# Top-sixteen selection by quarter of the sequence, the first quarter's beside the mixer's last quarter

## The chip, the cores and the metric

The kernel runs on one core of a Trainium2 chip. The metric is device time in microseconds (us), as the median of several runs. Five engines work side by side, each through its own instruction queue in order: TensorE (PE, matmuls), VectorE (DVE), ScalarE (ACT), GpSimd (POOL) and SyncE (SP), whose queue issues the DMA transfers.

## The reference

Two layers over a sequence of 1040 real columns (16 learned ones and 1024 inputs, width 1024). Each layer adds a mixer and then PEER, an expert network with product keys.

```python
for i in range(DEPTH):                       # DEPTH = 2
    h = h + hybrid_mixer(rms_norm(h, attn_norm[i]), ...)
    h = h + peer_ffn(rms_norm(h, ffn_norm[i]), ...)
return rms_norm(h[:, BLOCK:], final_norm)

def peer_ffn(xn, wq, sub_keys, u, v):
    q = (xt @ wq).reshape(t, PEER_HEADS, 2, PEER_HALF)          # 8 heads, two halves
    s = einsum('thpd,hpnd->thpn', q, sub_keys)                  # 64 scores for each head and half
    s_top, i_top = top_k(s, 16)
    cand_s = s_top[:, :, 0, :, None] + s_top[:, :, 1, None, :]  # sums of pairs
    best_s, best_j = top_k(cand_s, 16)
    g = softmax(best_s)
    h_all = einsum('td,nd->tn', xt, u)                          # all 4096 experts
    a = gelu(h_sel) * g                                         # h_sel: the 128 chosen ones of h_all
    w = zeros(t, 4096).at[arange(t), idx].add(a)
    return w @ v
```

The mixer is a sliding-window attention, a stick-breaking attention and a gated linear attention beside each other, each with a norm of its own, and an output projection.

## The kernel before

Matmuls run in a split of float32: each operand is a rounded part and a remainder, and a product takes three matmuls. A piece of weights that is used for the first time is copied by ACT (L272) and its remainder formed on POOL or DVE (L279, by the list that `split_on` set last); a piece that was kept comes back by DMA, with one ACT copy (L306).

The columns are cut in quarters of 272, 256, 256 and 256 (in layer 1 the first has 256 too). The mixer goes quarter by quarter (`attn_span`, in it `sbreak` with the scans L715 and the products L718, then `out_span`). PEER then works on two pairs of quarters, P (the first two) and Q (the last two). For a pair:
- `scores` (L977) gives the scores in four blocks c of two heads each; ACT moves them out of PSUM (L982).
- `route_steps` selects on DVE for the whole pair, one c after the other. `top16` is five instructions: maximum, index, replace, maximum, index (L994 to L998). It runs once for each tile of up to 128 columns, head and half of the keys (80 groups in P of layer 0, which has five tiles; 64 where there are four), and once for each tile and head on the sums of pairs (40 or 32 groups). Some thirty further instructions for each c turn positions into expert numbers and gates (an Exp on ACT, L1029; the products L1064 and L1067; the last steps L1079 to L1082). In the text the second top-sixteen and these are "the combination".
- `slots` transposes the result on PE (L1120, L1121, L1125); it needs all four c of the pair.
- `hidden` makes h_all row by row, 32 rows (L1101, with Gelu on ACT, L1110). `gates` (DVE L1140 to L1145, PE L1152) builds gates for 16 columns at a time; it needs the slots and is spread over the rows from `PR` = 17 on.
- `values` multiplies with v in two passes of 32 rows (L1191; operands by ACT L1185 and DVE L1186), then `hupdate` (L259) adds to h. During P's values, Q's scores and selection are mixed in, by a budget for each row (`BUD`, `EVERY`).

P's first-quarter scores for three of the four c in layer 0 (two in layer 1: `P.ns` is 4 there, and 3 of them) are issued in the mixer's last quarter, but selection on DVE starts only behind the mixer's last post-processing, `A.done`: the DVE instruction L598 of the last quarter.

A scheduler sets the order of the instructions of each engine when the program is built; the engines then keep to it. So an instruction that waits holds up what stands behind it on its engine. Tiles lie at fixed places in two large buffers, `arena` and `arena_r`, and the scheduler keeps those that overlap apart. While the mixer's last quarter runs, `widen` gives some of its tiles second or third buffers, in a place that the projections of earlier quarters no longer need.

## Time and profile before

| | us |
|---|---|
| median of 3 runs | 3345.01 |
| lowest and highest | 3344.48, 3348.84 |
| profiled execution | 3347.21 |
| its span in the trace | 3345.5 |
| PE busy | 3140.4 |
| DVE busy | 2107.7 |
| ACT busy | 1311.3 |
| POOL busy | 938.1 |

The profile is of one execution. Its own time is 1.7 us more than the span, which lies around the first and the last instruction. Busy times of the engines overlap. Times in the rows further down count from the span's start.

### The profile page before, as it was taken

How to read it: one execution, taken by the hardware profiler on the slowest of the kernel's cores; microseconds unless marked ns; L12 is line 12 of the kernel's file. 1: busy time of each engine (PE TensorE's matmuls, PEld its weight loads, DVE VectorE, ACT ScalarE, POOL GpSimd, SP SyncE). 2: the span in 40 equal slices, each digit the busy share in tenths (PEclk: the TensorE clock that was granted, in tenths of full speed). 3: DMA queues.
4: the chain of work that ended last, by engine and by line, in shares of the span. 5: the costliest groups of instructions: out<-in, count | busy, mean ns of one | idle time of the engine just before them, and what ended most of it. 6: DMA issues, size and time to landing. Idle time of an engine off the chain costs nothing.

```text
span 3345.5 us, 65752 instructions
## 1 busy us (share of the span) xinstructions
PE 3140.4 (94%) x23483; PEld 2642.3 (79%) x23483; DVE 2107.7 (63%) x6764; ACT 1311.3 (39%) x3021; POOL 938.1 (28%) x963
## 2 busy tenths in 40 slices
PE   7999999989799989999998999999898899999998
PEld 7686887679799988888875868876776778688788
DVE  4645436569997589653325464465697867975447
ACT  4544324433223434324344343245342244333345
POOL 4314021214344233010311131223143433311125
PEclk9899999989899999999997999999898999999999
DMA  8767774655335655446874677756754366554655
GB/s 290 228 208 245 238 261 135 199 188 187 124 117 158 183 178 190 155 152 200 311 251 151 216 263 238 253 160 201 233 177 139 115 181 219 182 187 145 194 177 160
DMA packets 397225, 651.36 MB, mean 195 GB/s; under 512 B 43536, under 2 KB 109152, under 8 KB 396896
## 3 DMA queue, kind: packets, MB, share of 16 engines
q1 hardware_dynamic: 396896, 647.16, 60.1%
q8 instruction: 184, 3.01, 0.4%
q14 instruction: 145, 1.19, 0.1%
HBM read 489.56 MB, written 157.42 MB: 193 GB/s over the span
## 4 chain that ended last, share of the span: by engine, by line
PE 61%; DVE 21%; DMA 6%; ACT 2%; issue 2%; POOL 1%; SPq 0%; DVEq 0%; POOLq 0%; ACTq 0%
PE b L1191 15%; PE b L1101 14%; PE b L333 11%; PE b L977 4%; PE b L1152 3%; PE b L703 2%; DVE arena_r L1186 2%; DMA arena<-h 2%; DVE arena L995 2%; DVE arena L996 2%; PE b L757 1%; DVE arena L998 1%; PE b L618 1%; DVE arena L1140 1%; DVE arena L1145 1%
## 5 line engine op out<-in xcount | busy, mean ns | idle before, releaser
L279 POOL TENSOR_TENSOR arena_r<-arena,arena_r 128x512 fp32r<-128x512 f32 (+1 forms) x453 | 557.6, 1238 | 915.0 <-ACT arena_r L272 843.8
L1101 PE MATMUL b<-arena_r 128*128 128x512 f32 (+2 forms) x3840 | 766.4, 359 | 22.9 <-ACT arena L1110 13.4
L1191 PE MATMUL b<-arena_r 128*128 128x512 f32 (+2 forms) x4224 | 752.5, 337 | 31.9 <-DVE arena_r L1186 22.1
L1191 PEld LDWEIGHTS b<-arena_r 128*128 128x128 f32 x4224 | 642.6, 190 | 128.9 <-DVE arena_r L1186 37.2
L1101 PEld LDWEIGHTS b<-arena_r 128*128 128x128 f32 x3840 | 630.7, 193 | 123.0 <-ACT arena L1110 14.0
L333 PE MATMUL b<-arena_r 128*128 128x256 f32 (+1 forms) x4992 | 700.9, 294 | 27.5 <-ACT arena_r L272 6.3
L333 PEld LDWEIGHTS b<-arena_r 128*128 128x128 f32 x4992 | 641.0, 195 | 67.1 <-issue 20.4
L272 ACT ACTIVATE arena_r<-arena 128x512 fp32r<-128x512 f32 x456 | 285.0, 629 | 447.3 <-PE b L1101 93.7
L1186 DVE TENSOR_TENSOR arena_r<-arena,arena_r 128x512 fp32r<-128x512 f32 (+2 forms) x352 | 258.1, 743 | 215.6 <-ACT arena_r L1185 214.8
L306 ACT ACTIVATE arena_r<-arena 128x512 fp32r<-128x512 f32 x284 | 178.5, 631 | 359.8 <-PE b L1191 118.0
L977 PE MATMUL b<-arena_r 128*128 128x256 f32 (+1 forms) x1632 | 219.1, 290 | 17.9 <-DMA arena_r<-m_0l 6.4
L977 PEld LDWEIGHTS b<-arena_r 128*128 128x128 f32 (+1 forms) x1632 | 204.2, 190 | 30.9 <-DMA arena_r<-m_0l 8.5
L1140 DVE TENSOR_TENSOR arena<-arena 128x2048 f16<-128x2048 f16 x129 | 172.4, 1338 | 59.7 <-PE b L1152 59.7
L1108 POOL TENSOR_TENSOR arena<-arena 128x272 f32<-128x272 f32 (+26 forms) x86 | 90.0, 1051 | 372.5 <-ACT arena L1159 177.5
L1185 ACT ACTIVATE arena_r<-arena 128x512 fp32r<-128x512 f32 (+2 forms) x352 | 171.8, 502 | 24.1 <-PE b L1191 24.1
L1152 PEld LDWEIGHTS <-arena 128*128 128x128 f16 x4128 | 144.9, 118 | 36.9 <-DVE arena L1145 20.8
L1152 PE MATMUL b<-arena 128*128 128x32 f16 x4128 | 154.0, 190 | 18.9 <-DVE arena L1145 18.8
L255 POOL TENSOR_TENSOR arena<-arena 128x256 f32<-128x256 f32 (+2 forms) x105 | 90.7, 864 | 260.5 <-ACT arena L254 256.0
L715 DVE TENSOR_TENSOR_SCAN arena<-arena,zf 128x384 f32<-128x384 f32 (+6 forms) x116 | 104.5, 904 | 82.0 <-ACT arena L710 81.0
L279 DVE TENSOR_TENSOR arena_r<-arena,arena_r 128x256 fp32r<-128x256 f32 (+1 forms) x187 | 98.0, 528 | 89.7 <-ACT arena_r L272 72.0
L421 ACT ACTIVATE arena<-b 128x256 f32<-128x256 f32 (+1 forms) x144 | 55.4, 385 | 212.3 <-PE b L333 211.8
L1157 DVE SCALAR_TENSOR_TENSOR arena<-b,arena 128x288 f32<-128x288 f32 (+21 forms) x129 | 63.7, 499 | 111.6 <-PE b L1152 111.6
(268 smaller groups left out, 3877.9 us busy)
## 6 DMA issues: line engine op xcount, KB each, us to landing
arena<-in_v_w_dram SPq DMA_DIRECT2D x288, 256.0 KB, 2.9
arena<-in_u_pk_dram SPq DMA_DIRECT2D x256, 256.0 KB, 3.0
arena_r<-a_0h SPq DMA_DIRECT2D x108, 256.0 KB, 3.6
arena_r<-a_0l SPq DMA_DIRECT2D x108, 256.0 KB, 3.9
arena_r<-a_1h SPq DMA_DIRECT2D x108, 256.0 KB, 3.0
arena_r<-a_1l SPq DMA_DIRECT2D x108, 256.0 KB, 3.5
arena<-m SPq DMA_DIRECT2D x92, 256.0 KB, 4.4
arena<-in_w_pk_dram SPq DMA_DIRECT2D x72, 256.0 KB, 4.3
```

What stands on the lines that cost most here:

```text
L272: ACT.activation(hi, src, AF.Copy)
L279: e.tensor_tensor(lo[:, a:b], src[:, a:b], hi[:, a:b].bitcast(F32), op=ALU.subtract)
L306: ACT.activation(hi, wload(src), AF.Copy)
L333: PE.matmul(ps, wt[:, ks], x.at(low, k, xo, sp.w), start=(k == 0 and i == 0), stop=(k == KT - 1 and i == 2))
L715: DVE.tensor_tensor_scan(keep[0:m, 0:wd][:, ::-1], keep[0:m, 0:wd][:, ::-1], zf[0:m, 0:1].to_broadcast([m, wd]), keep[0:m, wd:wd + 1], op0 ...
L977: PE.matmul(ps, yv(half, low, k, oo, m), wt[:, kk * 256:kk * 256 + 256], start=(k == 0 and i == 0 and e == 0), stop=(k == KT - 1 and i == ...
L1101: PE.matmul(ps, wt[:, ks], yv(h, low, k, 0, w // 2 if h is None else w), start=(k == 0 and i == 0), stop=(k == KT - 1 and i == 2))
L1140: DVE.tensor_tensor(Lh, iotaM.unsqueeze(1).to_broadcast([128, 4, 128, 4]), v4(P.mT, 128), op=ALU.is_equal)
L1152: PE.matmul(ps[:, i * 32:(i + 1) * 32], Lh[:, b, :, t], R[:, b, part, :, t], start=(part == 0), stop=(part == 1))
L1185: ACT.activation(ah, G[:, r, o:o + w], AF.Copy)
L1186: last = DVE.tensor_tensor(al, G[:, r, o:o + w], ah.bitcast(F32), op=ALU.subtract)
L1191: PE.matmul(ps, wt[:, d * 128:d * 128 + 128], pr[low], start=(opens and r == 0 and i == 0), stop=(closes and r == 31 and i == 2))
```

## The change

It does these things:
- `route_steps` becomes `tops` (the first top-sixteen) and `combine` (the second and all that follows). Both work on one half of a pair (one quarter) and on two of the four c at once (`cc`), so that a call has 12 or 8 groups in place of 10 or 8, and `NG` is 12.
- All of the first quarter's scores, and `tops` on them, are issued in the mixer's last quarter, ahead of `out_span`. They have a place of their own (`s0`, `V`, `I`), where `widen` had the mixer's extra buffers; `widen` now adds one tile `sel` and nothing else.
- `combine` of the first quarter follows `A.done`; the second quarter's `tops` and `combine` come behind its scores. `slots` is called for each half, and `gates` reads the half's own tiles.
- ACT moves two tiles of scores out of PSUM in one instruction. The rings of PSUM banks for hidden, gates and scores are changed.
- In P's values, Q's scores stand at rows 6, 12, 18 and 24 of the first pass, both norms at row 0; the selection's budget is 2.4 for each row of the first pass and 1.8 for the second, with the steps priced anew. Of Q's second half only `tops` are in it; its `combine` follows the first `HQ` = 8 (was 6) rows of Q's hidden, and gates are spread up to row 31 (`PEND`, was 29).
- `hload`, `hsq` and `hupdate` work by quarter. Layer 0's last values no longer put every fourth remainder on DVE. At the end of the kernel the final norm of the first three quarters is placed inside the value passes, and only the last quarter stays in SBUF.

```diff
-    wide = [("sel", 2), ("pc", 1), ("pp", 1), ("pmt", 1), ("osq", 1)]
     def widen():
-        o = place["qaT0"][1][0]
-        for t, n in wide:
...
+        place["sel"][1].append(o_in)
...
+    o1 = lay(1, [("s0", 1536, 1), ("V", 384, 2), ("I", 384, 2)], place["qaT0"][1][0])
...
+    def tops(P, half, cc):
+        nt = len(P.parts[half][1].tiles)
...
+        for a in range(8):
+            for j in range(nt):
+                top16(sv(P, half, 2 * cc + a // 4)[:, j, a % 4, :], V[:, j, a], I[:, j, a])
+                yield 1.3
+
+    def combine(P, half, cc, startT, pidxT):
+        nt = len(P.parts[half][1].tiles)
+        ng = 4 * nt
+        V, I = P.V.pop((half, cc))
...
             if q == 3:
-                for c in range(P.ns - 1):
-                    scores(l, P, c, (0,), "d")
+                for cc in range(2):
+                    for c in (2 * cc, 2 * cc + 1):
+                        scores(l, P, c, (0,), "d")
+                    run(tops(P, 0, cc))
                 rb = rstd(2 * l + 1, qs[1])
             out_span(l, L, A)
...
-        scores(l, P, P.ns - 1, (0,), "s")
         apply(2 * l + 1, qs[1], gf, Y[1], rb)
...
-        for c in range(P.ns):
+        with tc.issue_after(A.done):
+            run(combine(P, 0, 0, *tabs), combine(P, 0, 1, *tabs))
+        for c in range(4):
             scores(l, P, c, (1,), "s")
-            with tc.issue_after(A.done):
-                route(P, c, startT, pidxT)
+        slots(P, 0)
+        run(tops(P, 1, 0), combine(P, 1, 0, *tabs))
         hidden(l, P, G, 0, 4, "h")
...
+        run(tops(P, 1, 1), combine(P, 1, 1, *tabs))
+        slots(P, 1)
         hidden(l, P, G, 4, PR, "h")
-        slots(P)
         hidden(l, P, G, PR, 32, "h", cst, PEND)
...
+        work = {6 * c + 6: lambda c=c: scored.append(scores(l, Q, c, (0, 1), "g")) for c in range(4)}
+        work[0] = norms
+        todo = values(l, P, G, (0, 1), 0, select(), work, 2.4)
+        todo = values(l, P, G, (0, 1), 4, todo, (), 1.8)
+        run(todo)
         hidden(l, Q, G, 0, HQ, "h")
-        slots(Q)
+        run(combine(Q, 1, 0, *tabs), combine(Q, 1, 1, *tabs))
+        slots(Q, 1)
```

In the changed kernel `top16` is L996 to L1000 (was L994 to L998), the hidden matmuls L1113 (was L1101), the slots' transposes L1131, L1132 and L1136 (were L1120, L1121 and L1125), and the values' DVE operand L1197 (was L1186). Three places show the move.

DVE, layer 0, inside the last quarter of the mixer, before: scans and products of the stick-breaking attention with copies out of PSUM between them.

```order
L715 SCALAR_TENSOR_TENSOR arena<-arena,zf 128x512
L747 COPY arena<-b_69 128x512
L718 SCALAR_TENSOR_TENSOR arena<-arena 128x512
L715 SCALAR_TENSOR_TENSOR arena<-arena,zf 128x272
L718 SCALAR_TENSOR_TENSOR arena<-arena 128x272
L715 SCALAR_TENSOR_TENSOR arena<-arena,zf 128x400
```

The same stretch with the change, on the same engine:

```order
L1000 MAX_INDEX arena<-arena 128x8 x4
L715 SCALAR_TENSOR_TENSOR arena<-arena,zf 128x384
L1000 MAX_INDEX arena<-arena 128x8
L587 TENSOR_TENSOR arena<-arena,b_71 128x256
L1000 MAX_INDEX arena<-arena 128x8
L279 TENSOR_TENSOR arena_r<-arena,arena_r 128x256
L996 MAX arena<-arena 128x8
L718 SCALAR_TENSOR_TENSOR arena<-arena 128x384
L996 MAX arena<-arena 128x8 x3
L588 TENSOR_TENSOR arena<-arena 128x256
L997 MAX_INDEX arena<-arena 128x8 x4
L715 SCALAR_TENSOR_TENSOR arena<-arena,zf 128x272
```

All 240 instructions of the first quarter's first top-sixteen (48 groups) now stand ahead of `A.done`, and 160 (32 groups) in layer 1.

PE, layer 1, hidden rows of P around the transposes of the second quarter's slots, before; a row of hidden is 24 matmuls, and the rows above this place bring the hidden matmuls ahead of the first L1120 to 409 of 768.

```order
L1101 MATMUL b_72<-arena_r 128x512 x24
L1101 MATMUL b_65<-arena_r 128x512 x24
L1125 MATMUL b_67<-ident,arena 128x128
L1101 MATMUL b_66<-arena_r 128x512
L1120 LDWEIGHTS arena
L1120 MATMUL b_68<-ident_78,arena 128x128
L1101 MATMUL b_66<-arena_r 128x512
```

The same place with the change, where the count ahead of the first L1131 of the second half is 243:

```order
L1113 MATMUL b_68<-arena_r 128x512 x24
L1136 MATMUL b_65<-ident,arena 128x128
L1113 MATMUL b_71<-arena_r 128x512 x24
L1113 MATMUL b_72<-arena_r 128x512 x4
L1136 MATMUL b_65<-ident,arena 128x128
L1113 MATMUL b_72<-arena_r 128x512 x20
L1113 MATMUL b_67<-arena_r 128x512 x3
L1131 LDWEIGHTS arena
L1131 MATMUL b_66<-ident_78,arena 128x128
```

The transposes have moved 166 hidden matmuls forward on PE; in layer 0 they have moved from 816 of 1536 narrower ones to 510.

DVE, layer 1, from the last operand of P's values on, before:

```order
L1186 TENSOR_TENSOR arena_r<-arena,arena_r 128x512
L994 MAX arena<-arena 128x8 x4
L995 MAX_INDEX arena<-arena 128x8
L994 MAX arena<-arena 128x8 x3
L1058 COPY arena<-arena 128x8
L1059 TENSOR_TENSOR arena<-arena 128x15x8
L995 MAX_INDEX arena<-arena 128x8 x4
```

And with the change:

```order
L1197 TENSOR_TENSOR arena_r<-arena,arena_r 128x512
L996 MAX arena<-arena 128x8 x13
L997 MAX_INDEX arena<-arena 128x8
L996 MAX arena<-arena 128x8
L997 MAX_INDEX arena<-arena 128x8 x7
L1039 COPY arena<-arena 128x8
L997 MAX_INDEX arena<-arena 128x8 x4
```

Between this operand and Q's last slots DVE had 15 groups of top-sixteen and now has 40, in both layers; on PE the hidden matmuls of Q ahead of the first L1120 or of the second half's first L1131 were 174 and are 279 (278 in layer 0).

## Rows read from the trace of the kernel before

**Rows 1.** The page: engine busy times, and the group of remainders on POOL.
```profile
PE 3140.4 (94%) x23483; PEld 2642.3 (79%) x23483; DVE 2107.7 (63%) x6764; ACT 1311.3 (39%) x3021; POOL 938.1 (28%) x963
...
L279 POOL TENSOR_TENSOR arena_r<-arena,arena_r 128x512 fp32r<-128x512 f32 (+1 forms) x453 | 557.6, 1238 | 915.0 <-ACT arena_r L272 843.8
```

**Rows 2.** Windows: length; busy of PE, PEld, DVE, ACT, POOL; clock; DMA.
```profile
642.00:699.00 57.00, 50.87 (x372) 35.39 (x371) 31.92 (x65) 22.99 (x51) 11.99 (x26) 0.95 0.31 97
699.00:910.00 211.00, 179.57 (x1358) 174.35 (x1359) 194.05 (x1153) 69.68 (x139) 75.11 (x57) 0.92 0.56 183
910.00:1045.00 135.00, 129.40 (x1766) 127.40 (x1766) 114.86 (x149) 37.16 (x108) 65.47 (x49) 0.96 0.35 111
...
2290.00:2355.50 65.50, 60.68 (x484) 45.48 (x480) 37.17 (x75) 28.76 (x63) 23.25 (x35) 0.97 0.47 158
2355.50:2546.00 190.50, 160.63 (x838) 136.29 (x837) 167.54 (x960) 66.97 (x118) 66.07 (x52) 0.90 0.62 203
2546.00:2684.00 138.00, 123.13 (x1392) 102.81 (x1392) 105.64 (x141) 37.60 (x93) 61.73 (x42) 0.91 0.36 116
```

**Rows 3.** PE's waits, 680 to 1310: us in total, times, longest.
```profile
PE b L1191 <- DVE arena_r L1186: 11.1, 19, 1.6
PE b L1120 <- DVE arena L1080: 7.8, 1, 7.8
```

**Rows 4.** PE's waits, 2330 to 2960.
```profile
PE b L1152 <- DVE arena L1145: 13.3, 8, 3.0
PE b L1120 <- DVE arena L1080: 9.1, 1, 9.1
...
PE b L1191 <- DVE arena_r L1186: 7.6, 7, 2.2
```

**Rows 5.** DVE's timeline: `A.done` of each layer, and parts of top16.
```profile
698.18 0.69 DVE L598 TENSOR_TENSOR arena_r<-arena,arena_r 128x512 fp32r<-128x512 f32 x1 [0.76 <-ACT arena_r L597]
...
701.15 0.07 DVE L995 MATCH_VALUE_LOAD arena<-arena 128x8 f32 x1
...
702.70 0.07 DVE L995 MATCH_VALUE_LOAD arena<-arena 128x8 f32 x1
...
2354.90 0.69 DVE L598 TENSOR_TENSOR arena_r<-arena,arena_r 128x512 fp32r<-128x512 f32 x1 [0.76 <-ACT arena_r L597]
...
2355.90 1.22 DVE L994 MAX8 arena<-arena 128x8 f32<-128x64 f32 x9
```

**Rows 6.** DVE's waits, 699 to 910.
```profile
DVE arena L373 <- DMA arena<-h: 8.0, 3, 3.9
```

**Rows 7.** PE's timeline in P's hidden: start, us, idle before in brackets.
```profile
765.16 23.57 PE L1101 MATMUL b<-arena_r 128*128 128x272 f32 x192
...
908.29 0.19 PE L1120 MATMUL b<-ident,arena 16*128 16x16 f16 x1 [7.83 <-DVE arena L1080]
...
2426.38 72.47 PE L1101 MATMUL b<-arena_r 128*128 128x512 f32 x312
...
2544.91 0.29 PE L1120 MATMUL b<-ident,arena 128*128 128x128 f16 x1 [9.08 <-DVE arena L1080]
...
2567.52 2.31 PE L1152 MATMUL b<-arena 128*128 128x32 f16 x64
2569.68 5.58 PE L1101 MATMUL b<-arena_r 128*128 128x512 f32 x23
...
2683.73 6.48 PE L1191 MATMUL b<-arena_r 128*128 128x512 f32 x15 [1.56 <-ACT arena_r L1185]
```

**Rows 8.** One copy of the combination by form, 2355 to 2546 and 2690 to 2960.
```profile
L1080 DVE COPY arena<-arena 128x128 f16<-128x128 f16 x4 | 4.6, 1154 | 0.0
...
L1080 DVE COPY arena<-arena 128x128 f16<-128x128 f16 x3 | 1.4, 457 | 0.0
```

**Rows 9.** Timelines of DVE and PE, from P's last values to Q's slots, layer 1.
```profile
2923.21 0.87 DVE L1186 TENSOR_TENSOR arena_r<-arena,arena_r 128x512 fp32r<-128x512 f32 x1
...
2967.33 0.23 PE L1120 MATMUL b<-ident,arena 128*128 128x128 f16 x1
```

**Rows 10.** Windows: the first projection of layer 1.
```profile
1604.00:1690.00 86.00, 76.52 (x513) 69.64 (x513) 26.66 (x49) 32.43 (x64) 37.69 (x37) 0.96 0.97 344
```

More of the change, by code (lines that the diff above doesn't have):

```diff
@@ L1111, in hidden, with slots @@
             P.rows = r + 1
-            while cst and P.gated < P.sp.w and P.gated * (end - lo) < P.sp.w * (r + 1 - lo):
-                gates(P, G, *cst)
-    def slots(P):
-        sp = P.sp
-        for j, (o, m) in enumerate(sp.tiles):
+            while cst and sum(P.gated) < P.sp.w and sum(P.gated) * (end - lo) < P.sp.w * (r + 1 - lo):
+                gates(P, int(P.gated[0] == P.parts[0][1].w), G, *cst)
+    def slots(P, half):
+        for j, (o, m) in enumerate(P.parts[half][1].tiles):
             tp = ps1("g").bitcast(F16)[:, 0:256].rearrange("p (a b) -> p a b", a=2)
@@ L1305, in tile_trunk @@
-        work += [lambda c=c: scores(l, Q, c, (0, 1), "d") for c in range(4)]
-        step = 0
-        done = []
-        for d in (0, 4):
-            for last in values_steps(l, P, G, (0, 1), d):
-                done.append(last)
-                step += 4
-                if work and step >= EVERY:
-                    work.pop(0)()
-                    step = 0
-                    if len(work) < 4:
-                        todo = itertools.chain(todo, route_steps(Q, 3 - len(work), startT, pidxT))
-                if len(work) < 4:
-                    left = BUD * 4
-                    with tc.issue_after(done[-1 - LAG]):
-                        while left > 0:
-                            left -= next(todo, 9)
@@ L1322, in tile_trunk, with norms, select @@
-        for _ in todo:
-            pass
-        split_on(POOL)
+        Q = peer_setup(qs[2], qs[3], False)
+        scored = []
+        def norms():
+            apply(2 * l + 1, qs[2], gf, Y[0], rb)
+            apply(2 * l + 1, qs[3], gf, Y[1], rb2)
+        def select():
+            for half in range(2):
+                for cc in range(2):
+                    for gen in (tops(Q, half, cc), combine(Q, half, cc, *tabs) if half == 0 else iter(())):
+                        while len(scored) < 2 * cc + 2:
+                            yield 99
+                        yield from gen
+                if half == 0:
+                    slots(Q, 0)
@@ L1344, in tile_trunk, with final @@
             continue
-        hs = sb([128, KT, 512], F32, "s")
-        for k in range(KT):
-            SP.dma_start(hs[:, k], hv[2 * l + 1][k][:, Q.sp.c0:Q.sp.c1])
-        values(l, Q, G, (0, 1), 0, hs)
-        split_on((POOL, DVE))
-        for sp in qs[0:2]:
+        def final(sp):
             rb = rstd(2 * DEPTH, sp)
```

264 lines of the change are left out of this document (137 added, 127 removed).

## The prediction

> **What bounds the kernel now.** I read the page first, then busy times by stretch, PE's waits, and the timelines around those waits. PE is busy for 3140.4 us of the 3345.5 [rows 1], so only its idle time and its clock can give much. In PEER the idle time lies around P's selection: PE is idle for 31 us of the 211 between the mixer's end and the slots of layer 0, and for 30 of the 190 in layer 1 [rows 2]. In those two stretches DVE is busy for 194 and 168 us: selection bounds them. PE could run hidden rows ahead, but its order puts the transposes at a fixed place, and there it stands and waits, 7.8 us in layer 0 and 9.1 in layer 1, for the last steps of the combination [rows 3, 4]. Behind the slots PE bounds (129.4 us busy of 135, and 123.1 of 138) [rows 2], except that in layer 1 the last gates come one by one behind the last hidden row, for which PE waits 13.3 us [rows 4].
>
> So P's end is a chain of three: `A.done`; from there DVE's work up to the slots; then what PE still has to do behind the slots. The change touches all three.
>
> **A.done.** It stands at 698.9 and 2355.6 (start and length of L598) [rows 5]. 48 groups of top-sixteen come ahead of it in layer 0 and 32 in layer 1. A group's price: a load of match values with its index or replace takes (702.70 - 701.15) / 8 = 0.194 us, a maximum 1.22 / 9 = 0.136 [rows 5], so three of the first and two of the second make 0.85 us. That is 41 and 27 us. The stretch before `A.done` had 31.9 us of DVE work in 57, and 37.2 in 65.5 [rows 2]. In layer 0, 31.9 + 41 = 73 is 16 more than fits; I take **18 later**. In layer 1, 37 + 27 = 64 would just fit, but only if the order left no hole, and the scans wait for ACT and PE in between; I take **9 later**. Bounds: 16 and 0 if every hole is filled, 41 and 27 if none is. Score matmuls that move into the mixer lay behind `A.done` before; they are not new work for PE. The loss of the extra mixer buffers is within these bounds: it makes holes.
>
> **From A.done to the slots.** The stretch loses these groups: 194 - 41 = 153 us of DVE work in layer 0 and 168 - 27 = 140 in layer 1. Before, DVE also idled there, 17 and 23 us [rows 2]; 8.0 of it in layer 0 was the load of h for the norm [rows 6], while top-sixteen of the first quarter waited its turn behind. The combination of a quarter that is already scored can lie under these loads, so I take 2 and 3 us of idle: **155 and 143**. Bounds: 153 and 140 with none; 170 and 163 with all the old idle. PE can keep up: 510 hidden matmuls at 23.57 / 192 = 0.123 us are 63 us in layer 0, 243 at 72.47 / 312 = 0.232 are 56 in layer 1 [rows 7].
>
> **Behind the slots.** The price of earlier slots is that more of hidden is left. Layer 0: 1536 - 510 = 1026 matmuls at 0.1228 = 126 us, and 33 blocks of gates with 32 matmuls at (2569.68 - 2567.52) / 64 = 0.0338 [rows 7] = 36; with 2 us of small waits, **164**. Layer 1: 525 at 0.2323 = 122, and 32 blocks = 35; with 2, **159**. The gates now run to row 31 among hidden matmuls, so the 13.3 us of waiting has no place; that is in these numbers. Before, the same pieces were 1045 - 908 = 137 and 2684 - 2545 = 139 [rows 2, 7].
>
> Together: layer 0 ends P's hidden at 698.9 + 18 + 155 + 164 = 1036 against 1045, **-9**; layer 1 at 2355.6 + 9 + 143 + 159 = 2666.6 against 2683.7, **-17**.
>
> **Values of P.** PE waits there for its low operand (L1186), 11.1 and 7.6 us [rows 3, 4], which queues on DVE behind pieces of selection. With the change less selection lies in these passes (below), so I take **-14** of the 18.7; bounds 0 and -18.7.
>
> **Q's second half.** What leaves the values comes behind them. From the last L1186 of P's values to Q's slots DVE took 44 us (2923.21 to 2967.33), and PE 174 x 0.2323 = 40 us of hidden and about 4 of values; nobody waited [rows 7, 9]. With the change DVE has 25 more groups (21 us), about half as much again of the other steps (12 by the ratio of their number) and two gate blocks (4): 44 + 37 = 81. PE now has 279 matmuls ahead, 65 + 4 = 69. So a new wait of 12 at most appears; DVE's 44 may hold some idle time, so I take 8 in each layer, **+16** (bounds 0 and +24). This is where the stall goes.
>
> **The rest.** The first projection of layer 1 loses DVE's share of its remainders. POOL was busy for 37.7 of these 86 us [rows 10], at 1.24 us for each [rows 1]; every fourth one in the layer's last values falls to it too. POOL stays below half full on average, but pieces come in bursts: **+3**, between 0 and +8. More and smaller loads and updates of h, ACT's merged score copies, the banks and the final norms inside the values lie under PE-bound values and POOL's 72% of idle time [rows 1]: **0**; without that cover the last norm alone could cost about 3.
>
> **Sum** against the profiled execution: 3347.2 - 9 - 17 - 14 + 16 + 3 = 3326 (3325.3 unrounded). The profiled run is 2.2 us over the median of those shown, so **3323**.
>
> **Two rules against the trace.** The same 128x128 copy of the combination took 1154 ns between 2355 and 2546 and 457 later in the values [rows 8]. The Trainium skill, "GPSIMD Engine Reference", section 8, Key points, says that GpSimd shares its interfaces to SBUF with VectorE and contends with some of its instructions; by that rule the moved selection is as slow beside POOL's work in the mixer as before. The trace agrees that the price depends on the stretch, and in layer 1 POOL works in 35% of the old selection and of the mixer's last quarter alike [rows 2], so the sum stays as it is. The clock in P's stretches was 0.90 to 0.92 where PE idled most and 0.95 to 0.97 where it idled less [rows 2]. The Trainium skill, "TensorE: Matmul & The Clock Gate", HAM oscillation, warns that pauses between bursts bring the lower clock back. The trace's clocks agree; since one pause before the slots stays and the late gates' pauses go, I put it at 0, between -8 and +8.
>
> **The rivals.**
> *More is gained.* Q's slots don't wait, the values lose all 18.7, and the combination leaves no hole: 3323 - 16 - 5 - 5 = 3297. If three steps of each of the four combinations also cost 0.7 us less, as in the values [rows 8], 17 more over both layers: 3280. For it: DVE idles a third of the time [rows 1]. Against it: Q's count of matmuls.
> *Nothing is gained.* DVE's order has holes again: the second quarter's scores come only after the norm, and what stands behind a waiting instruction waits as well. All the old idle time costs 15 + 20 = 35 us: 3358; half of it, about 3339. For it: 17 and 23 us of idle were there before although work was at hand [rows 2]. Against it: the combination needs nothing from the second quarter.
> *Slower.* The mixer's last quarter is serialised: with single buffers and top-sixteen in DVE's queue ahead of the scans, none of the moved 68 us fits into holes. Then `A.done` is 41 and 27 later, 41 more than I take: 3364. It decides from a total delay of about 27 + 22 = 49 us. For it: DVE's order stands fixed and the scans' chain runs over DVE, ACT and PE; against it: 25 and 28 us of DVE idle time lie in these stretches [rows 2].
>
> **How the numbers follow.** Forecast (3305 to 3338) 0.52; more gained (3280 to 3305) 0.18; nothing gained (3338 to 3358) 0.17; slower (3355 to 3385) 0.13. A measurement of this kernel tells 0.2%, or 6.7 us, from no change. Faster than 3338.3: the first two, 0.70. Within: most of the third and a little of the fourth, 0.14. Slower: the rest, 0.16. The range 3284 to 3348 leaves out 0.2, most of it above.
>
> **What would show it.** After: `A.done` near 717 and 2365; the last transposes of the second half 155 and 143 us later; no gates behind the last hidden row; values from about 1036 and, from `A.done`, 302 us later in layer 1; a wait of some 8 us for DVE at Q's second slots. The forecast is wrong if the mixer's last quarter grows by more than 25 us in a layer, if DVE idles over 10 us before the slots, or if the values' operand waits stay.

## The result: slower by 0.65%

The changed kernel took 3369.05 us (median of 4 runs, 3366.37 to 3373.87) against 3346.93 for the kernel before on the same chip (4 runs). The ratio is 1.0065 with a 95% interval of 1.0046 to 1.0084. The profiled span grew from 3345.5 to 3372.2 us, by 26.7. On other chips the kernel before had medians of 3350.9 to 3353.1 us, so experiments are compared below by their ratio to it on the same chip, and by stages of their profiles. A profile is one execution; a stage of one kernel repeats within some 5 us.

The page of the changed kernel says at first sight that nothing happened: PE has the work of before, DVE 40 us less, in a longer span.

```profile
PE 3139.0 (93%) x23453; PEld 2643.3 (78%) x23453; DVE 2067.2 (61%) x6737; ACT 1309.9 (39%) x3005; POOL 946.3 (28%) x966
```

The loss has to be read by stages. I took them from the timelines, each from the start of the first instruction to the start of the next stage's first; "third A.done" is that of the mixer's third quarter.

| stage | before | after | change | forecast |
|---|---|---|---|---|
| layer 0: third `A.done` to the last | 142.8 | 169.2 | +26.4 | +18 |
| to P's values | 347.2 | 319.6 | -27.5 | -27 |
| P's values, to their last matmul | 261.0 | 255.9 | -5.1 | -7 |
| to Q's values | 216.5 | 228.3 | +11.8 | +8 |
| to layer 1's third `A.done` | 700.0 | 708.2 | +8.1 | +3 |
| layer 1: to the last `A.done` | 132.1 | 153.7 | +21.6 | +9 |
| to P's values | 328.8 | 308.5 | -20.4 | -26 |
| P's values | 246.1 | 240.2 | -5.8 | -7 |
| to Q's values | 213.6 | 225.2 | +11.6 | +8 |
| to the end | 202.1 | 207.7 | +5.7 | 0 |

The rows of the changed kernel that answer to `A.done` in [rows 5], on DVE's timeline:

```profile
724.90 0.69 DVE L598 TENSOR_TENSOR arena_r<-arena,arena_r 128x512 fp32r<-128x512 f32 x1 [0.76 <-ACT arena_r L597]
...
2390.53 0.69 DVE L598 TENSOR_TENSOR arena_r<-arena,arena_r 128x512 fp32r<-128x512 f32 x1 [0.76 <-ACT arena_r L597]
```

And those that answer to [rows 2], windows with the columns given there, cut at the new `A.done`, the second half's first transposes and the start of P's values:

```profile
642.00:725.60 83.60, 70.64 (x508) 53.28 (x505) 73.25 (x455) 29.80 (x61) 15.46 (x33) 0.91 0.38 114
725.60:876.00 150.40, 121.95 (x896) 117.69 (x895) 145.87 (x778) 49.12 (x98) 49.84 (x35) 0.89 0.60 194
876.00:1044.50 168.50, 166.57 (x2086) 165.03 (x2087) 114.33 (x138) 48.30 (x134) 80.46 (x61) 0.98 0.42 134
2284.00:2391.00 107.00, 94.83 (x693) 66.06 (x689) 81.45 (x362) 47.02 (x101) 31.16 (x43) 0.93 0.52 164
2391.00:2529.00 138.00, 114.03 (x627) 98.78 (x626) 134.00 (x712) 47.44 (x86) 42.64 (x34) 0.88 0.63 205
2529.00:2699.00 170.00, 158.86 (x1555) 132.26 (x1554) 111.82 (x134) 49.15 (x116) 81.78 (x59) 0.96 0.46 144
```

In layer 0, DVE's 73.25 us of work in the mixer's last stretch are the 31.9 of [rows 2] and the 41 of the moved groups, and the stretch that held 57 us is now 83.6 long. Behind it selection is as short as forecast (150.4 us, DVE busy for 145.9). But add PE's idle time over the three stretches: before 6.1 + 31.4 + 5.6 = 43 us, now 13.0 + 28.5 + 1.9 = 43. It has only moved. What layer 0 gained behind `A.done` it had paid ahead of it. The windows of layer 1 do not begin at the same place (67 us behind the third `A.done` in [rows 2], 47 here), but the whole way from the third `A.done` to P's values says the same of both layers: PE is idle for 50.8 us before and 52.3 after in layer 0, and for 55.2 and 54.1 in layer 1.

The rows that answer to [rows 7] and [rows 9], PE's timeline: the transposes of the second half, the last gates of layer 1, the start of P's values, and Q's first hidden rows.

```profile
876.21 0.23 PE L1131 MATMUL b<-ident,arena 128*128 128x128 f16 x1 [2.14 <-DVE arena L1092]
...
1044.52 1.67 PE L1203 MATMUL b<-arena_r 128*128 128x272 f32 x12
...
1299.73 0.96 PE L1203 MATMUL b<-arena_r 128*128 128x256 f32 x7
1310.08 2.50 PE L1113 MATMUL b<-arena_r 128*128 128x512 f32 x5 [9.40 <-DVE arena L259]
...
2529.34 0.23 PE L1131 MATMUL b<-ident,arena 128*128 128x128 f16 x1 [0.31 <-DVE arena L1092]
...
2692.35 1.25 PE L1164 MATMUL b<-arena 128*128 128x32 f16 x32 [1.73 <-DVE arena L1157]
2695.98 1.24 PE L1164 MATMUL b<-arena 128*128 128x32 f16 x32 [2.38 <-DVE arena L1157]
2699.00 1.22 PE L1203 MATMUL b<-arena_r 128*128 128x512 f32 x2 [1.77 <-ACT arena_r L1196]
...
2949.41 2.08 PE L1113 MATMUL b<-arena_r 128*128 128x512 f32 x4 [2.94 <-DVE arena L259]
```

Q is late by the forecast's amount and more, but not at the slots: PE stands for 9.40 us at Q's first hidden row and waits for an update of h. The forecast has no such wait.

### The profile page after: what moved, and what is told of

Read it like the earlier page. It is cut to its first block, busy times and chain, and to the rows that moved or that the text cites. A ratio compares the mean times of both kernels' runs of the same rounds, so it can differ in the third digit from the quotient of the medians.

```text
span 3372.2 us, 65688 instructions
## 1 busy us (share of the span) xinstructions
PE 3139.0 (93%) x23453; PEld 2643.3 (78%) x23453; DVE 2067.2 (61%) x6737; ACT 1309.9 (39%) x3005; POOL 946.3 (28%) x966
## 4 chain that ended last, share of the span: by engine, by line
PE 60%; DVE 20%; DMA 7%; ACT 2%; issue 2%; POOL 1%; SPq 1%; POOLq 0%; DVEq 0%; ACTq 0%
PE b L1113 17%; PE b L1203 14%; PE b L333 11%; PE b L1164 3%; PE b L987 3%; DMA arena<-h 2%; PE b L703 2%; DVE arena L998 2%; DVE arena L997 2%; DVE arena_r L1197 2%; DVE arena L1000 1%; PE b L757 1%; PE b L618 1%; DVE arena L999 1%; DVE arena L1152 1%
## 5 line engine op out<-in xcount | busy, mean ns | idle before, releaser
L279 POOL TENSOR_TENSOR arena_r<-arena,arena_r 128x512 fp32r<-128x512 f32 (+1 forms) x440 | 551.6, 1260 | 896.9 <-ACT arena_r L272 820.2
L1203 PE MATMUL b<-arena_r 128*128 128x512 f32 (+2 forms) x4224 | 751.7, 338 | 29.8 <-DVE arena_r L1197 20.9
L1113 PE MATMUL b<-arena_r 128*128 128x512 f32 (+2 forms) x3840 | 758.6, 357 | 14.4 <-DVE arena L259 12.3
L1113 PEld LDWEIGHTS b<-arena_r 128*128 128x128 f32 x3840 | 626.6, 191 | 112.6 <-DVE arena L259 13.0
L1197 DVE TENSOR_TENSOR arena_r<-arena,arena_r 128x512 fp32r<-128x512 f32 (+2 forms) x352 | 271.9, 787 | 293.7 <-ACT arena_r L1196 292.3
L987 PE MATMUL b<-arena_r 128*128 128x256 f32 (+1 forms) x1632 | 217.0, 289 | 10.6 <-DMA arena_r<-m_0l 3.5
L987 PEld LDWEIGHTS b<-arena_r 128*128 128x128 f32 (+1 forms) x1632 | 202.5, 188 | 22.6 <-issue 4.4
L255 POOL TENSOR_TENSOR arena<-arena 128x256 f32<-128x256 f32 (+1 forms) x126 | 106.7, 847 | 286.8 <-ACT arena L254 285.6
L1196 ACT ACTIVATE arena_r<-arena 128x512 fp32r<-128x512 f32 (+2 forms) x352 | 171.9, 502 | 27.5 <-PE b L1203 22.8
L1120 POOL TENSOR_TENSOR arena<-arena 128x192 f32<-128x192 f32 (+23 forms) x81 | 89.3, 1109 | 329.0 <-ACT arena L1171 225.9
L1164 PEld LDWEIGHTS <-arena 128*128 128x128 f16 x4128 | 144.5, 118 | 26.4 <-issue 13.4
L1169 DVE SCALAR_TENSOR_TENSOR arena<-b,arena 128x304 f32<-128x304 f32 (+19 forms) x129 | 65.7, 516 | 153.6 <-PE b L1164 153.6
L421 ACT ACTIVATE arena<-b 128x256 f32<-128x256 f32 (+1 forms) x144 | 55.2, 384 | 200.0 <-PE b L333 199.4
L279 DVE TENSOR_TENSOR arena_r<-arena,arena_r 128x256 fp32r<-128x256 f32 (+1 forms) x140 | 77.9, 562 | 77.0 <-ACT arena_r L272 69.2
```

Source lines behind the costliest of these rows:

```text
L255: POOL.tensor_tensor(acc, acc, sq[:, 0:sp.w], op=ALU.add)
L279: e.tensor_tensor(lo[:, a:b], src[:, a:b], hi[:, a:b].bitcast(F32), op=ALU.subtract)
L987: PE.matmul(ps, yv(half, low, k, o, m), wt[:, kk * 256:kk * 256 + 256], start=(k == 0 and i == 0 and e == 0), stop=(k == KT - 1 and i == 2 ...
L1113: PE.matmul(ps, wt[:, ks], yv(h, low, k, 0, w // 2 if h is None else w), start=(k == 0 and i == 0), stop=(k == KT - 1 and i == 2))
L1164: PE.matmul(ps[:, i * 32:(i + 1) * 32], Lh[:, b, :, t], R[:, b, part, :, t], start=(part == 0), stop=(part == 1))
L1196: ACT.activation(ah, G[:, r, o:o + w], AF.Copy)
```

## The experiments

Fourteen runs were made: thirteen edited kernels, and the changed kernel once more. Theories at the start: the mixer's last quarter is late because top-sixteen stands in DVE's queue ahead of the scans (1), or because the mixer lost its extra buffers (2); the rest is late through half-width updates of h, or through the selection that is left behind the values.

**a1: top-sixteen behind A.done.** Edit of the changed kernel:

```diff
             if q == 3:
-                for cc in range(2):
-                    for c in (2 * cc, 2 * cc + 1):
-                        scores(l, P, c, (0,), "d")
-                    run(tops(P, 0, cc))
+                for c in range(2):
+                    scores(l, P, c, (0,), "d")
...
         with tc.issue_after(A.done):
-            run(combine(P, 0, 0, *tabs), combine(P, 0, 1, *tabs))
+            run(tops(P, 0, 0))
+        for c in range(2, 4):
+            scores(l, P, c, (0,), "s")
+        with tc.issue_after(A.done):
+            run(tops(P, 0, 1), combine(P, 0, 0, *tabs), combine(P, 0, 1, *tabs))
```

> The changed kernel with the first quarter's top-sixteen behind A.done again and the scores of only two of its four c in the mixer; the lost buffers stay lost. Measure: from A.done of the mixer's third quarter to that of its last, before 142.8 and 132.1 us (layers 0 and 1), after 169.2 and 153.6. Theory 1 (top-sixteen stands in DVE's queue ahead of the mixer's scans): back to 139 to 147 and 128 to 136. Theory 2 (the lost buffers): stays above 160 and 147. The selection's chain behind A.done grows by about 41 and 27 us again, so the time is some 20 us above the changed kernel by theory 1 (3389), some 60 above it by theory 2.

The stretches came back to 142.9 and 134.7 us with the buffers still lost, so theory 2 is out. The time was not above the changed kernel but below it, 1.0018 (1.0001 to 1.0035) of the kernel before. DVE's timeline, PE's around the slots and values of layer 0, and the windows:

```profile
698.81 0.69 DVE L598 TENSOR_TENSOR arena_r<-arena,arena_r 128x512 fp32r<-128x512 f32 x1 [0.76 <-ACT arena_r L597]
...
2352.30 0.69 DVE L598 TENSOR_TENSOR arena_r<-arena,arena_r 128x512 fp32r<-128x512 f32 x1 [0.76 <-ACT arena_r L597]
```

```profile
890.73 0.23 PE L1131 MATMUL b<-ident,arena 128*128 128x128 f16 x1 [1.60 <-DVE arena L1092]
...
1028.13 2.05 PE L1203 MATMUL b<-arena_r 128*128 128x272 f32 x15
```

```profile
642.00:699.00 57.00, 50.56 (x362) 35.77 (x361) 31.01 (x62) 22.80 (x49) 10.36 (x23) 0.88 0.29 93
699.00:891.00 192.00, 169.41 (x1283) 162.66 (x1284) 191.59 (x1164) 67.85 (x132) 74.75 (x55) 0.95 0.63 201
891.00:1028.00 137.00, 134.54 (x1845) 132.72 (x1845) 115.14 (x136) 39.33 (x114) 66.95 (x51) 1.00 0.40 126
```

Theory 1 does not follow from a1 alone, because the edit takes two things out of the mixer: top-sixteen, and score matmuls of PE. In layer 0 the stretch between the third and the last `A.done` holds 144 of these before (20.4 us), 288 in the changed kernel (38.9) and 144 in a1; in layer 1 144 (20.9 us), 192 (26.1) and 96. (`P.ns` is 3 in layer 0, so two c were in the mixer before, and 4 in layer 1, so three: the section on the kernel before has the two layers the wrong way round.) What the traces add is the chain that ended last in the mixer's last stretch, by its lines: layer 0 before (642 to 699), then with the change (642 to 725.6), and layer 1 with the change (2284 to 2391).

```profile
by line: PE b L977 21.2%; PE b L703 17.1%; PE b L757 14.1%; PE b L739 11.2%; PE b L580 4.5%; POOL arena L576 2.9%; DVE arena L715 2.7%; PE b L333 2.5%; PE b L570 2.5%; POOL arena L356 2.4%; issue 1.9%; ACT arena_r L597 1.7%; DVE arena L591 
...
by line: DVE arena L715 15.4%; DVE arena L997 11.7%; DVE arena L998 10.5%; DVE arena L1000 9.7%; DVE arena L999 7.2%; DVE arena L996 7.0%; DVE arena L718 6.2%; DVE arena L747 3.8%; DVE arena_r L279 3.8%; PE b L757 3.4%; PE b L580 2.4%; POOL
...
by line: PE b L987 14.2%; PE b L703 12.3%; PE b L757 8.8%; PE b L739 5.7%; PE b L333 5.0%; DMA arena<-m 4.5%; PE b L391 4.1%; DMA m<-arena 3.0%; PE b L580 2.8%; PE b L570 2.6%; DVE arena L998 2.2%; PE b L822 2.2%; PE b L396 2.0%; DVE arena 
```

In layer 0 the chain has gone over from PE to DVE, and 46% of the stretch is top-sixteen (L996 to L1000) between the scans: theory 1. In layer 1 it has stayed on PE, with the scores (L987) as its largest part. There theory 1 is not shown; PE's busy time in the whole stretch grew by 13.2 of the 21.6 us, part of it by the 48 score matmuls more and part by a lower clock (0.98 before, 0.94 after). No run moved the scores alone.

The selection is 41 us longer again (191 us from `A.done` to the second half's transposes), and yet P's values start at 1028.1, 16 us ahead of the changed kernel and 17 ahead of the kernel before. PE uses the longer selection for hidden rows (169 us busy of 192), so that only 137 us of work are left behind the slots and not 168; over the three stretches PE idles for 6.4 + 22.6 + 2.5 = 31 us. Moving 41 us out of the selection was worth 329.3 - 319.6 = 9.7 us behind `A.done`, and cost 26.3 ahead of it. So in layer 0 what the change does behind `A.done` is a gain, and the place beside the mixer is the loss. The gain shows in a wait that [rows 3] leaves out. First the kernel before: ACT stood at the Exp of the combination (L1029), and PE at hidden rows for the Gelu (L1110) that stands behind it in ACT's queue, in total and at one place; then PE's wait for the Gelu in a1.

```profile
ACT arena L1029 <- DVE arena L1028: 33.7, 4, 11.8
PE b L1101 <- ACT arena L1110: 13.4, 3, 5.6
...
815.43 0.34 ACT L1029 ACTIVATE arena<-arena 128x160 f32<-128x160 f32 x1 [8.02 <-DVE arena L1028]
...
817.60 0.67 ACT L1110 ACTIVATE arena<-b 128x272 f32<-128x272 f32 x2
...
PE b L1113 <- ACT arena L1122: 2.6, 1, 2.6
```

Layer 1 had no such wait for a Gelu and gains next to nothing: from the third `A.done` to P's values it took 460.9 us before, 459.4 in a1 and 462.9 in d2 below.

**a2: the kernel before without the extra buffers.**

```diff
-    wide = [("sel", 2), ("pc", 1), ("pp", 1), ("pmt", 1), ("osq", 1)]
+    wide = [("sel", 1)]
```

> The kernel before, with one extra buffer sel in the mixer's last quarter in place of six extra buffers, and nothing else changed. Theory 1: the stretches stay at 142.8 and 132.1 within 3 us and the time at that of before within 0.2%. Theory 2: they grow by 15 us or more each, to above 158 and 147, and the time rises by 30 us or more.

142.5 and 142.9 us: no loss in layer 0, 10.8 in layer 1; 1.0015 (0.9995 to 1.0035). But layer 1's stretch was also 141.5 in c4 below, which keeps all buffers and edits nothing near the mixer, and of the kernels that have lost the buffers a1, b2, c3 and d2 had 134.6 to 135.9 and b3 and c2 143.3 and 144.9. Much of this is TensorE's clock. Those six have the same 880 matmuls there; the granted clock, a mean of its two levels, was 0.94 to 0.97 in the four and 0.90 and 0.88 in the two, and PE's busy time 119 to 120 and 127 to 129 us. The kernel before had 0.98, a2 0.94 and c4 0.91. So a price of the buffers in layer 1 is not shown; in layer 0 there is none beyond the 5 us that a stage varies by.

**a3: updates of h in one piece.**

```diff
+        if w > 272:
+            for i in range(2):
+                hsq(ver, k, Span(sp.c0 + 256 * i, sp.c0 + 256 * i + 256), ht[:, 256 * i:256 * i + 256])
+            return
         hsq(ver, k, sp, ht)
...
+                if h is None and hs is None:
+                    hupdate(2 * l + 2, d0 + d, P.sp, hload(2 * l + 1, d0 + d, P.sp), ps)
+                    continue
```

> The changed kernel, but h is loaded, updated and stored for merged pairs of quarters in one piece of 512 columns again (squares by halves). Theory: twice as many loads through three tiles arrive late, so layer 1's first projections and mixer start late; from the end of layer 0's last values matmul to the last update of h it takes 11 us after the change and 7 before. It goes back to 7 or 8, and the time falls by 5 to 10 us below the changed kernel (3359 to 3364). Rival: the updates are hidden; within 3 us of the changed kernel.

The last updates of layer 0 on DVE's timeline, first in the changed kernel (its last values matmul starts at 1791.4), then in a3 (1796.3):

```profile
1795.74 0.42 DVE L259 TENSOR_TENSOR arena<-arena,b 128x256 f32<-128x256 f32 x1 [4.19 <-DMA arena<-h]
...
1798.17 0.42 DVE L259 TENSOR_TENSOR arena<-arena,b 128x256 f32<-128x256 f32 x1 [0.52 <-DMA arena<-h]
1801.21 0.88 DVE L259 TENSOR_TENSOR arena<-arena,b 128x256 f32<-128x256 f32 x2 [2.15 <-DMA arena<-h]
```

```profile
1802.79 0.69 DVE L259 TENSOR_TENSOR arena<-arena,b 128x512 f32<-128x512 f32 x1 [1.25 <-DMA arena<-h]
```

From the last matmul to the start of the last update, 10.2 us became 6.5, as before the change. Q's stage in layer 1, behind a merged pair too, fell from 225.2 to 218.9, and not in layer 0 (229.5), where P's updates were halves before as well. The ratio was 1.0015 (0.9995 to 1.0035), 0.5% below the changed kernel, a larger gain than these 10 us. The profiled execution (span 3364.5) is one of the longer of its ten; the rest is not accounted for.

**a4: updates ahead of the leftover selection.**

```diff
-        run(todo)
+        with tc.issue_after(updated[-1]):
+            run(todo)
...
-        run(combine(Q, 1, 0, *tabs), combine(Q, 1, 1, *tabs))
+        with tc.issue_after(updated[-1]):
+            run(combine(Q, 1, 0, *tabs), combine(Q, 1, 1, *tabs))
```

> The changed kernel, but what is left of Q's selection when P's values end stands behind the last update of h on DVE. Theory: Q's first hidden rows wait for PSUM banks that the updates free, and these stand in DVE's queue behind top-sixteen: the wait of PE on L259 there, 9.4 and 2.9 us, falls below 3 us in layer 0 and the time by 5 to 10 us (3359 to 3364). Rival: DVE's amount of work up to Q's second slots is the limit: the wait only moves to the slots or gates, within 3 us of the changed kernel.

1.0093 (1.0063 to 1.0122). The wait on the update fell from 9.4 to 5.1 us in layer 0, but the slots of the second half came at 1408 and not at 1377, and Q's stages grew to 240.6 and 239.6. With the order forced this way 65 groups of top-sixteen come behind the last operand of the values, and not 40, and PE's idle time in layer 0's stage doubled from 9.4 to 18.1 us, most of the new part before slots and gates. The forecast of a faster kernel failed.

**b0: the changed kernel again.**

> The changed kernel once more, so that the others of this call have it on the same chip. Every theory: 1.004 to 1.009 of the kernel before.

1.0070 (1.0048 to 1.0093); its stages repeat those of the table within 5 us.

**b1: no debt in the budget.** A step that finds its scores missing answers 99, and the change subtracts that from a running sum, so that the first values pass does no selection.

```diff
-                        left -= next(todo, 99)
+                        n = next(todo, 99)
+                        left = 0.0 if n == 99 else left - n
```

> The changed kernel, but a step of the selection that answers that its scores are not there yet (the answer is 99) ends the row's budget in place of being subtracted from it. With the subtraction the first pass starts at -97 and earns 2.4 a row, so it does no selection over its 32 rows: the trace shows one group of top-sixteen between 1045 and 1160 us, and 40 are left behind the values. Theory: this debt is what puts 40 groups behind the values and makes Q's hidden late. From the end of P's values to Q's values it took 228.3 us in layer 0 and 225.2 in layer 1 after the change, 216.4 and 213.6 before: back to 219 and 216 or less, and the time 15 to 25 us below the changed kernel. Rival: DVE's work in the values grows, and PE's waits for the low operand there grow by as much; within 6 us of the changed kernel.

As few groups were left behind the values as in the kernel before, some 15 and not 40, and Q's stages stayed at 227.7 and 224.8. PE waits as before at Q's first row:

```profile
1318.33 2.05 PE L1113 MATMUL b<-arena_r 128*128 128x512 f32 x4 [9.62 <-DVE arena L259]
```

The time was 1.0097 (1.0070 to 1.0124); P's values were 5 us longer in each layer than in the changed kernel. The debt is there, but the number of groups that it leaves is not what makes Q late: the theory fell.

**c4: the kernel before with shared banks.** Before, Q's hidden used PSUM banks 0, 1, 6 and 7, and P's values 2 to 7. After, hidden has 6, 7, 2 and 3, all of them banks of the values. Here the first two rows use the ring x, banks 6 and 7.

```diff
-        hidden(l, Q, G, 0, HQ, "h")
+        hidden(l, Q, G, 0, 2, "x")
+        hidden(l, Q, G, 2, HQ, "h")
```

> The kernel before, with the first two rows of Q's hidden on banks 6 and 7, which P's values use, and nothing else changed. Theory of the shared banks: PE waits on L259 for 6 to 11 us at Q's start in layer 0 and 2 to 6 in layer 1, which it did not before, and the time rises by 8 to 15 us. Rival: the updates come early enough when DVE has less selection left (15 groups and not 40): waits under 3 us, time within 0.2% of before.

Q's stages grew from 216.5 and 213.6 to 225.2 and 222.1, and the time to 1.0043 (1.0029 to 1.0058). PE's timeline around the end of P's values in layer 0, first in the kernel before, where hidden rows start between the values and run on behind them, then in c4:

```profile
1296.60 0.63 PE L1101 MATMUL b<-arena_r 128*128 128x512 f32 x2
...
1306.49 10.13 PE L1101 MATMUL b<-arena_r 128*128 128x512 f32 x43
1316.93 1.40 PE L1101 MATMUL b<-arena_r 128*128 128x512 f32 x5 [0.31 <-DVE arena L259]
```

```profile
1299.78 6.10 PE L1191 MATMUL b<-arena_r 128*128 128x256 f32 x49
1307.14 0.73 PE L1101 MATMUL b<-arena_r 128*128 128x512 f32 x2 [1.26 <-ACT arena_r L306]
1309.64 3.44 PE L1101 MATMUL b<-arena_r 128*128 128x512 f32 x10 [1.76 <-DMA arena_r<-u_0l]
1314.96 5.32 PE L1101 MATMUL b<-arena_r 128*128 128x512 f32 x16 [1.89 <-DVE arena L259]
```

The waits on the update are short (1.9 and 3.4 us, below what I expected of layer 0), and the rest of the 8.7 us goes with the overlap of hidden and values, which is gone. Before, the last updates stood as late on DVE (1316.0, 10 us behind the values) and PE hardly waited, since its first rows had banks of their own. In the changed kernel the wait is longer, 9.40 us; selection stands between the updates on DVE there, and a4, which puts the updates first, has 5.1.

**c1: free banks for two rows of the changed kernel.** The ring d is banks 0 and 1.

```diff
-        hidden(l, Q, G, 0, HQ, "h")
+        hidden(l, Q, G, 0, 2, "d")
+        hidden(l, Q, G, 2, HQ, "h")
```

> The changed kernel, with the first two rows of Q's hidden on PSUM banks 0 and 1, which P's values don't use (as in the kernel before), in place of banks that the last update of h has to free. Theory: sharing all of hidden's banks with the values is what makes Q late. PE's wait on L259 there (9.4 us in layer 0, 2.9 in layer 1) goes away; from the end of P's values to Q's values 218 to 221 us in layer 0 (changed kernel 228, before 216) and 221 to 224 in layer 1 (225, before 214); time 9 to 14 us below the changed kernel. Rival: the leftover selection bounds Q, as I had predicted; then PE waits at the second half's slots instead and the stage stays within 2 us of 228 and 225.

1.0175 (1.0156 to 1.0194), stages 247.7 and 248.2: worse, by neither theory. PE's wait for an update, which was to go, rose to 11.9 us in layer 0 and went in layer 1 alone, and PE waited 5.3 and 15.7 us at the transposes of the gates (L1136) in the two layers. Banks 0 and 1 also serve the slots of Q's first half, which the change issues among the values and finishes late, so that the edit adds a conflict of its own, which I did not follow further. It told nothing of the question.

**d1: the banks of before for all of Q.**

```diff
+    hq=(0, 1, 6, 7), gq=(2, 3)
...
-                if half == 0:
-                    slots(Q, 0)
...
-        hidden(l, Q, G, 0, HQ, "h")
+        hidden(l, Q, G, 0, 4, "hq")
+        slots(Q, 0)
+        hidden(l, Q, G, 4, HQ, "hq")
```

Q's scores go to the ring d, its slots and gates to gq, its later rows to hq.

> The changed kernel with the PSUM banks of the kernel before for Q: its hidden rows on banks 0, 1, 6 and 7, its scores on 0 and 1, its slots and gates on 2 and 3, and for that the slots of Q's first half out of the values to behind four rows of hidden (banks 2 and 3 belong to the values until then). Theory: banks shared with the values cost 8 to 9 us in each layer (they did when put into the kernel before). From the end of P's values to Q's values 217 to 221 us in layer 0 and 214 to 218 in layer 1 (changed kernel 228 and 225); time 14 to 22 us below the changed kernel, 1.001 to 1.003 of the kernel before. Rival: the leftover selection on DVE bounds Q once the banks don't; then PE waits for the slots and the stages stay above 224.

Besides the banks, this moves the slots of Q's first half from the values to behind four rows of hidden; c4 changes banks alone. Q's stages fell to 218.3 and 220.1, with 40 groups still left behind the values; the time fell to 0.9992 (0.9980 to 1.0004). Hidden rows run between the values and on behind them again:

```profile
1291.61 0.86 PE L1114 MATMUL b<-arena_r 128*128 128x512 f32 x3
1292.30 6.12 PE L1204 MATMUL b<-arena_r 128*128 128x272 f32 x48
1298.27 10.61 PE L1114 MATMUL b<-arena_r 128*128 128x512 f32 x45
1309.73 2.60 PE L1114 MATMUL b<-arena_r 128*128 128x512 f32 x10 [0.85 <-DVE arena L259]
```

Another 10 us of its gain lie between Q's values of layer 0 and layer 1's third `A.done` (698.2 us and not 708.2), where nothing was edited.

**b2, b3, c2, c3, d2: mends together.** b2 is a1, a3 and b1 in one; b3 is b2 with the final norms issued between the passes and not inside; c2 is a1, a3 and c1; c3 is c2 with both quarters of the last pair kept in SBUF as before; d2 is a1, a3, d1 and c3's end.

> Three mends together: top-sixteen of the first quarter behind A.done and two c of its scores in the mixer, h loaded, updated and stored whole for merged pairs, and no debt in the budget. If the three theories hold and add up: A.done within 4 us of before, P's values start 10 to 17 us earlier than before in layer 0, Q's hidden as before; span near 3322, a ratio of 0.990 to 0.996 to the kernel before. If the gain of the late top-sixteen was taken back by something else: 0.998 to 1.002.

> The same three mends, and the final norms of the first three quarters issued between the value passes of the end in place of within them. Theory: the norms inside the last passes take DVE's time from the low operands, whose waits doubled there (3.4 to 6.6 us), and the end took 26.6 us of 214.8 more than before is not all theirs but some 4 us: 3 to 6 us below the kernel with three mends. Rival: the scheduler puts them into the same holes; within 2 us.

> Three mends of the changed kernel together: top-sixteen of the first quarter behind A.done with two c of its scores in the mixer, h loaded, updated and stored whole for merged pairs, and free banks for the first two rows of Q's hidden. If each keeps what it gave alone: A.done as in the kernel before within 4 us in both layers, P's values 13 to 18 us earlier than before in layer 0, Q's stages 217 to 221; span 3325 to 3335, ratio 0.993 to 0.998 to the kernel before. If they take from each other: 0.998 to 1.002.

> The same three mends, and both quarters of the last pair kept in SBUF and normed from there at the end, as in the kernel before (the first two quarters' norms stay within the passes). Theory: the first of them by way of DRAM is what the end costs: from the start of layer 1's last values to the end of the kernel 202 us before and 207 to 211 in the kernels with the new end. Back to 201 to 204. Rival: the order of the passes' own operands costs it; no change within 2 us.

> Four mends of the changed kernel: top-sixteen of the first quarter behind A.done with two c of its scores in the mixer; h loaded, updated and stored whole for merged pairs; the old banks for Q; both quarters of the last pair normed from SBUF at the end. If each keeps what it gave alone: A.done as before within 4 us, P's values 13 to 18 us earlier in layer 0 and 3 to 8 in layer 1, Q's stages 214 to 221, the end 202 to 204; span 3315 to 3330, ratio 0.990 to 0.996. If not: 0.997 or more.

b2: 0.9999 (0.9981 to 1.0017), the second case: P's values start 18 us ahead of the kernel before in layer 0, and Q's stages, 229.0 and 220.3, take it back. b3: 1.0047 (1.0031 to 1.0064); the end took 217.6 us against 206.7 in b2, so the norms inside the passes are the better place, against my theory. PE's wait for the low operand there rose from 7.2 to 11.3 us. c2 (1.0092, 1.0073 to 1.0111) and c3 (1.0102, 1.0085 to 1.0120) missed their forecasts, since they carry c1's loss at each Q, 31 to 35 us over the kernel before. c3's end took 203.1 us and c2's 207.8. The five kernels that norm the whole last pair from SBUF (the kernel before, a2, c4, c3 and d2) took 202.1 to 204.4 us there, and the others, without b3, 206.7 to 211.6, so the new end costs some 5 us. c3 puts back more than the half that went by DRAM, though: also the place of its norm and the division of the remainders between POOL and DVE. Which of the three costs it is open. d2 beats both kernels: 0.9939 (0.9922 to 0.9957), 3330.13 us median of 11 runs. Two of its rows, DVE's timeline at layer 0's last `A.done` and PE's at P's values:

```profile
700.40 0.69 DVE L603 TENSOR_TENSOR arena_r<-arena,arena_r 128x512 fp32r<-128x512 f32 x1 [0.76 <-ACT arena_r L602]
```

```profile
1036.29 3.90 PE L1209 MATMUL b<-arena_r 128*128 128x272 f32 x30
```

Its P's values start 9 us ahead of the kernel before in layer 0, short of the 13 expected; Q's stages are 218.0 and 213.3 us, the end 204.4, the span 3334.6 (3315 to 3330 expected).

## Why the prediction was wrong

I forecast 3323 us, with a range of 3284 to 3348, and faster with a chance of 0.70. By the table the forecast of the profile was -21 us and the measured change +26.7. Of the 48 us between them 21 lie ahead of `A.done`, 5 from there to P's values, 3 in P's values, 7 at Q and 11 in the rest. Step by step:

- **"A.done ... I take 18 later ... 9 later": mis-sized.** Measured 26.4 and 21.6, so the mixer's last quarter grew by more than the 25 us that I had named as a sign of being wrong. Both lie inside the bounds (16 to 41, 0 to 27), and I chose near the lower end. In layer 0 the chain to `A.done` shows the cause: idle DVE time between scans was counted as room, though a scan behind a run of top-sixteen instructions waits for it. The Trainium skill, "Perfetto Trace Analysis", Tensor Engine Instruction, has DVE as strictly first in, first out; the chain of layer 0, with 46% of the stretch in top-sixteen between the scans, agrees. The sum priced `A.done` by DVE's work alone: the score matmuls that move ahead of it are "not new work for PE" in all, but PE's busy time in the two stretches grew by 18.3 and 13.2 us. In layer 1 the chain runs over PE, and how the delay divides between scores, clock and top-sixteen is open.
- **"From A.done to the slots ... 155 and 143": near**, 150.6 and 138.1. **"Behind the slots ... 164 and 159": near in layer 0** (168.3), 11 short in layer 1 (169.7): "the 13.3 us of waiting has no place" was wrong, since gates still come behind the last hidden row and PE waited there for 8.0 us.
- **What this was worth: the idea under the forecast failed.** I let the shorter selection count as gain and noted that more hidden is left. The two terms are the same work of PE. With PE's idle time as long after as before in both layers, the stages could only trade: P's end came 1 us earlier in layer 0 and 1 us later in layer 1, counted from the third `A.done`, and not 9 and 17 earlier. In layer 0 a1 gains because it takes idle time out of the selection without adding any in the mixer, and most of that was the wait for the Gelu, 13.4 us, which the forecast did not read: it named only the 7.8 at the slots.
- **"Values of P ... -14": right in sign**, -11.
- **"Q's second half ... +16": near in size by chance, wrong in cause.** The loss is 23.4, at Q's first row and not at the slots. b1 has the old number of groups left and the same loss; c4 and d1 show the banks, which I had put among "the banks ... 0". In layer 1 the half-width loads of h share in it (a3).
- **"The rest ... +3" and 0: mis-sized.** 8.1 up to layer 1's third `A.done`, of which 3.8 go with late updates (a3), and 5.7 at the end, of which 4.7 go with the new end (c3 against c2).
- **The rival "Slower"** named the place, and for layer 0 the mechanism. It was to decide from a total delay of 49 us; the delay was 48 of the 68 that it moves, and the unpriced edits did the rest. (Half of the 35 us of "Nothing is gained" gives 3340.5 and not 3339; nothing rests on it.)
- **The two rules.** For selection beside POOL's work the sum was left as it was. The change gave rows for it. L1092 answers to the line of [rows 8]; of its two copies for layer 0's second quarter one ran while POOL formed remainders (L279) and one just behind them. Timelines of DVE and POOL:

```profile
858.32 1.38 DVE L1092 COPY arena<-arena 128x128 f16<-128x128 f16 x1
...
875.72 0.44 DVE L1092 COPY arena<-arena 128x128 f16<-128x128 f16 x1
...
853.97 5.43 POOL L279 TENSOR_TENSOR arena_r<-arena,arena_r 128x512 fp32r<-128x512 f32 x3 [6.84 <-ACT arena_r L272]
...
873.90 1.64 POOL L279 TENSOR_TENSOR arena_r<-arena,arena_r 128x512 fp32r<-128x512 f32 x1 [0.56 <-ACT arena_r L272]
```

The Trainium skill, "GPSIMD Engine Reference", section 8, Key points (shared interfaces of GpSimd and VectorE), agrees with that. The moved groups themselves do not feel POOL: over the whole trace a maximum on 64 scores took 208 ns (mean) beside a remainder of POOL and 212 without, an index 215 both times, a replace 207 and 205. So the sum was right to stay, but for another reason than the one given, that the selection is as slow in the mixer as before.

The clock was 0.88 and 0.89 in the stretches where PE idled most and 0.96 and 0.98 behind the slots; over the whole span it was 0.959 and before 0.961, so the 0 held. Idle time alone does not set it: in layer 0's mixer stretch PE idled for 21.9 us here, at 0.94, and for 18.8 in b0, the same kernel, at 0.88, and took 169.2 and 174.1 us.

Open: why a3 gained more in time than its profile shows, what the delay of layer 1's `A.done` is made of and what the lost buffers cost there, and why the clock of its mixer differs from kernel to kernel.

## What to carry to other kernels

When a stage's bound is a chain on a second engine, shortening the chain pays only if the main engine was idle beside it; add up the main engine's idle time over all the stages that the work moves between, and count what the move adds to each queue that it moves into, the main engine's too. Price "harmless" edits by what they let overlap: for PSUM banks ask which phase holds each bank when the next phase starts, since a phase whose banks all belong to the one before must wait until that one's results are read out of them. A change of several parts is worth undoing part by part: four mends of this one, chosen by stage, turned 0.65% slower into 0.6% faster, nearly all of it in layer 0 and in P's values.

## What I had not expected of the hardware

Halving a transfer hardly shortened its wait: the loads of h of 128 KB took 2.9 us to land (median), those of 256 KB before had taken 3.7 and those of 128 KB there 3.4, and twice as many through the same three tiles left the last update 10.2 us behind the values and not 6.5.

A neighbour can triple a copy on DVE, 0.44 us with POOL still and 1.38 beside its remainders, and leave the maximum of top-sixteen as it is (212 and 208 ns).
